# The convolution's pointwise weights multiplied with the output projection's lower half on the chip

## The chip, the cores and the metric

One core of a Trainium2 chip runs the whole layer as one program. TensorE multiplies matrices, VectorE (DVE) and ScalarE (ACT) do elementwise work, GpSimd (POOL) takes some of it, and DMA engines move data between HBM and the on-chip memories; SP, ScalarE and GpSimd issue transfers, each in its own order. The metric is the time of one execution of the program in microseconds (us). Before the change three runs took 2019.04, 2021.59 and 2022.71 us.

## The reference

One decoder layer over 2048 tokens of 1024 channels, in float32. A combined projection makes q, k, v and the input of a gated convolution; sliding-window attention and the convolution run side by side; their results are concatenated and go through one output projection; a SwiGLU feed-forward network follows. Norms stand around both halves. The part that the change touches:

```python
def conformer_conv(u, conv_dw, conv_dw_b, conv_ln_g, conv_ln_b, w_conv_pw):
    a, gate = jnp.split(u, 2, axis=-1)
    h = a * jax.nn.sigmoid(gate)
    h = lax.conv_general_dilated(h, conv_dw[:, None, :], ..., feature_group_count=D_CONV) + conv_dw_b
    h = jax.nn.silu(layer_norm(h, conv_ln_g, conv_ln_b))
    return h @ w_conv_pw
...
mixed = jnp.concatenate([attn_out, conv_out], axis=-1) @ w_out
h = h + rms_norm(mixed, mix_post_g)
```

`w_conv_pw` is 512 x 512, `w_out` 1024 x 1024. Its upper 512 rows meet the attention's output, its lower 512 rows the convolution's.

## The kernel before

**Precision.** Every float32 operand of a product is split into a high part (a copy to fp32r, on ScalarE) and a low part (the difference, on VectorE or GpSimd). `three` issues three products for each pair: high by high, high by low, low by high. `split_w` (L129) is the helper for weights. A tile of the kind "hl" or "chl" holds both parts of a 128 x 512 block.

**Stages.** The tokens are four tiles of 512 (t = 0 to 3). For each tile there are: A (the projections, 14 units of 24 products), B (attention), T (the 31 convolution taps, on VectorE), C (the convolution's tail) and W (the output projection, the norm and the residual). The feed-forward network treats two tiles at a time by a Strassen-like scheme: F0 and G0 for tiles 0 and 1, F2 and G2 for tiles 2 and 3. In the trace the letter after "@" is the stage.

**What sets the order.** One stage at a time runs as the main one; others are pumped beside it from lanes (`Lane`), each with a rate in units of the main stage's own clock. Lane `ld` holds the tails C0 and C1, and lane `lw` holds C2, W2, C3 and W3, which run beside G0. A scheduler then orders the instructions of each engine once, when the program is built, by priority and by its own estimate of time. On the chip each engine works through its list strictly in that order, and an instruction that waits holds up all that follow it on its engine. This holds for SP's list of transfers too.

**Buffers.** Tiles of one kind share a fixed number of buffers (`BUFS`, L53): 8 "hl", 3 "fc", 2 "gb", 1 "wx", 1 "yt", 5 "chl". A tile that is asked for waits until an earlier one is read for the last time. In PSUM there are four banks "mm", three "tr" and one "ct"; all of the tail's work goes through "ct".

**The tail** (`conv_tail`, L592). After the LayerNorm, four blocks of channels are turned (four transposes each), then activated: tanh (L613), scale and shift (L615), and one VectorE instruction (L616) that leaves twice the swish. Each is split (L618 on ScalarE, L619 on GpSimd). Then for each of four output blocks m the pointwise weights are loaded (L625) and split, 12 products go into "ct" (L628), ScalarE halves the result (L630) and stores it from its own queue to `mixT` (L631), from which W loads it (L715).

**The output projection** (`stage_w`, L697) takes the eight blocks of `mixT` in four groups of two, and loads and splits the weights `w_out` for each; W0 also stores their low parts (`lo_out`), which the other three load.

**Norms of the next tiles.** In A1, `row_norms` (L264) loads eight blocks of 128 rows of x (tiles 2 and 3) into buffers of the kind "hl" (L271), squares and sums them on ScalarE (L272), and computes the inverse root on VectorE and GpSimd (`rsqrt`, L159 to L162). `norm_x` (L289) spreads this over a diagonal (L301, tile "gb"), turns it on TensorE (L306), and `split_x` makes A2's operands, of the kind "hl" again. The hooks at L402 say after which unit of A1 each of these is emitted.

Of the kernel before, what the change touches and what calls it, by code (L numbers as in the profile page):

```python
# [12 lines left out]
F32 = mybir.dt.float32  # L13
F32R = mybir.dt.float32r
# [3 lines left out]
AF = mybir.ActivationFunctionType  # L18
ALU = mybir.AluOpType
# [4 lines left out]
D = 1024  # L24
DFF = 2816
P = 128
T = 512
# [10 lines left out]
def layer_kernel(ctx, tc, x, xT, cols, rows, sinks, relb, onehot, w_in, w_pw, w_out, w_gate, w_up, w_down, out):  # L38
    nc = tc.nc
# [4 lines left out]
    dr = ctx.enter_context(tc.tile_pool(name="dr", bufs=1, space=DRAM))  # L44

    uid = [0]
    lab = ["X0"]

    def nm(s):
        uid[0] += 1  # L50
        return f"{s}@{lab[0]}_{uid[0]}"
# [3 lines left out]
    def t_(tag, shape, dt=F32):  # L55
        return sb.tile(list(shape), dt, tag=tag, name=nm(tag), bufs=BUFS[tag])

    def f4(tag, shape=(P, D)):
        return t_(tag, shape)

    def f2(tag, shape=(P, T)):
        return t_(tag, shape)

    def hl(tag):
        return t_(tag, (P, 2, T), F32R)

    def sm(n, dt=F32):
        kind = "A" if lab[0][0] == "G" else lab[0][0]
        return sb.tile([P, 8], dt, tag="sm" + kind, name=nm("sm"), bufs={"C": 8, "W": 4}.get(kind, 16))[:, 0:n]

    def bank(tag, bufs):
        return ps.tile([P, T], F32, tag=tag, name=nm(tag), bufs=bufs)
# [3 lines left out]
    ct = lambda: bank("ct", 1)  # L76


    act = nc.scalar.activation
# [23 lines left out]
    ptt = nc.gpsimd.tensor_tensor  # L103
# [3 lines left out]
    def mat(*args, **kw):  # L107
        r = nc.tensor.matmul(*args, **kw)  # L108
        if not inlane[0]:
            lead_pe[0] = r  # L110
        return r
# [17 lines left out]
    def split_w(raw, tag, low=None, made=False, on_pool=True):  # L129
        w = tag if not isinstance(tag, str) else hl(tag)  # L130
        if made:
            nc.sync.dma_start(w[:, 1].bitcast(F32), low)
        act(w[:, 0], raw, AF.Copy)  # L133
        if not made:
            (ptt if on_pool else vtt)(w[:, 1], raw, w[:, 0].bitcast(F32), ALU.subtract)
            if low is not None:
                (nc.gpsimd if on_pool else nc.sync).dma_start(low, w[:, 1].bitcast(F32))
        return w

    def weight(src, low, made, raw=None, on_pool=True):  # L140
        if raw is None:
            raw = t_("raw", (P, 2, T))
            nc.sync.dma_start(raw, src)
        return [split_w(raw[:, n], "w", low[n], made, on_pool) for n in range(2)]
# [43 lines left out]
    def three(o, pairs, first=True, last=True):  # L188
        n = 3 * len(pairs)
        i = 0  # L190
        for (sh, sl), (mh, ml) in pairs:
            for a, b in ((sh, mh), (sh, ml), (sl, mh)):
                mat(o, a, b, start=first and i == 0, stop=last and i == n - 1)
                i += 1
# [34 lines left out]

    mixT = dr.tile([KC, P, S], F32, name="mixT")  # L230
    h_scr = dr.tile([S, D], F32, name="h_scr")

    neg = cst.tile([P, 1], F32, name="neg")
    nc.vector.memset(neg, NEG)
# [15 lines left out]
    started = set()  # L250
# [292 lines left out]
    def conv_in(t, c):  # L543
        g = t_("glu", (P, 576))[:, 0 : HALO + T]
        if t == 0:
            nc.vector.memset(g[:, 0:HALO], 0.0)
            nc.sync.dma_start(g[:, HALO:], glu_scr[c, :, 0:T])
        else:
            nc.sync.dma_start(g, glu_scr[c, :, t * T - HALO : (t + 1) * T])
        y = f2("fc")  # L550
        vts(y, g[:, 0:T], dwh[:, c, 0:1], dwb[:, c : c + 1], ALU.mult, ALU.add)
        return g, y
# [10 lines left out]
    def stage_taps(t):  # L563
        L = f"C{t}"
        for c in range(4):
            while f"g{t}{c}" not in started:
                yield None
            lab[0] = L
            g, y = conv_in(t, c)
            for j in range(1, TAPS):  # L570
                stt(y, g[:, j : j + T], dwh[:, c, j : j + 1], y, ALU.mult, ALU.add)
                yield 0.68
                lab[0] = L
            nc.sync.dma_start(y_scr[c, :, t * T : (t + 1) * T], y)
            yield 0.68
# [16 lines left out]
    def conv_tail(t, yt):  # L592
        L = f"C{t}"
        lab[0] = L
        mv = sm(8).rearrange("p (s a) -> p s a", a=2)
        for s in range(4):
            st = sm(6)
            nc.vector.bn_stats(st, yt[:, s])
            nc.vector.bn_aggr(mv[:, s], st)
        r = rsqrt(mv[:, :, 1], 4, 1.0)  # L600
        nmr = sm(4)
        stt(nmr, mv[:, :, 0], -1.0, r, ALU.mult, ALU.mult)
        yield YL if t < 2 else YL2
        lab[0] = L
        for s in range(4):
            act(yt[:, s], yt[:, s], AF.Identity, scale=r[:, s : s + 1], bias=nmr[:, s : s + 1])
        sc = []
        for c in range(4):
            b = ct()
            for s in range(4):  # L610
                nc.tensor.transpose(b[:, s * P : (s + 1) * P], yt[:, s, c * P : (c + 1) * P], ident)
            th = f2("fc")
            act(th, b, AF.Tanh, scale=lnh[:, c : c + 1], bias=lnh[:, 4 + c : 5 + c])  # L613
            v = f2("fc")
            act(v, b, AF.Identity, scale=ln_g[:, c : c + 1], bias=ln_b[:, c : c + 1])  # L615
            stt(v, th, 1.0, v, ALU.add, ALU.mult)  # L616
            h = hl("chl")
            act(h[:, 0], v, AF.Copy)  # L618
            ptt(h[:, 1], v, h[:, 0].bitcast(F32), ALU.subtract)  # L619
            sc.append(h)  # L620
            yield 2
            lab[0] = L
        for m in range(4):
            raw = f2("fc")
            nc.sync.dma_start(raw, w_pw[m])  # L625
            w = split_w(raw, "mb" if t == 1 and m % 2 else "chl").rearrange("p a (k c) -> p a k c", c=P)
            o = ct()
            three(o, [((w[:, 0, k], w[:, 1, k]), (sc[k][:, 0], sc[k][:, 1])) for k in range(4)])  # L628
            z = f2("gb" if t > 1 else "fc")
            act(z, o, AF.Copy, scale=0.5)  # L630
            nc.scalar.dma_start(mixT[4 + m, :, t * T : (t + 1) * T], z)  # L631
            yield 2
            lab[0] = L

    bias = []

# [60 lines left out]
    def stage_w(w, spill, G, atag, htag, mtag, bank_of, norm=None, ready=None):  # L697
        L = f"W{w}"
        lab[0] = L
        acc = [f4(atag) for _ in range(4)]  # L700

        def acts(gi, ms=None):
            aa = []
            for m in ms or load(gi):
                a = hl(htag)
                act(a[:, 0], m, AF.Copy)  # L706
                vtt(a[:, 1], m, a[:, 0].bitcast(F32), ALU.subtract)
                aa.append([a])
            return aa

        def load(gi):
            ms = []
            for c in range(G * gi, G * gi + G):
                ms.append(f2(mtag))
                nc.sync.dma_start(ms[-1], mixT[c, :, w * T : (w + 1) * T])  # L715
            return ms

        first = load(0)
        if w != 1:
            yield 5.0  # L720
            lab[0] = L
        nxt = acts(0, first)
        for gi in range(KC // G):
            aa = nxt
            for n in range(2):
                lab[0] = L
                if n == 0 and w != 1 and gi + 1 < KC // G:
                    rows_next = load(gi + 1)
                if n == 1 and gi + 1 < KC // G and not (ready and G * gi + G == 4):
                    nxt = acts(gi + 1, rows_next if w != 1 else None)  # L730
                ws = weight(w_out[2 * gi : 2 * gi + 2, :, n * T : (n + 1) * T].rearrange("c p t -> p c t"),
                            lo_out[n, 2 * gi : 2 * gi + 2], w > 0)
                yield from block_half(acc, list(zip(aa, ws)), n, gi == 0, L, bank_of)
            if ready and G * gi + G == 4:
                for i, c in enumerate(ready()):
                    if i == Q0 // 2:
                        ld.until("C1")
                        lab[0] = L
                        nxt = acts(gi + 1)
                    yield c  # L740
        tail = norm_w(w, spill, acc, mtag)
        if norm:
            norm(tail)
        else:
            yield from tail
# [601 lines left out]
    ld = Lane(2.0, 0)  # L1347
# [23 lines left out]
    hn_a = {0: split_x(0, x0, None, range(KC))}  # L1371
    for t in range(NT):
        lc.add(f"T{t}", stage_taps(t))
    for t in range(2):
        ld.add(f"C{t}", stage_tail(t), lambda t=t: since(lc, f"T{t}", CS))
    for t in range(NT):
# [38 lines left out]
    ws, ops = (0, 1), {}  # L1415
# [12 lines left out]
    ws, ops = (2, 3), {}  # L1428
# [76 lines left out]
```

## Time and profile before

| | |
|---|---|
| runs | 2019.04, 2021.59, 2022.71 us; median 2021.59 |
| span of the profiled execution | 2016.4 us |
| instructions | 27154 |
| TensorE busy | 1957.8 us, 97% |
| VectorE busy | 1489.5 us, 74% |
| ScalarE busy | 985.7 us, 49% |
| GpSimd busy | 355.0 us, 18% |

The span runs from the program's first instruction to its last; the time of the profiled execution itself is not listed beside it. A row of a stretch reads: the stretch, its length, then for each engine (TensorE's products, its weight loads, VectorE, ScalarE, GpSimd) the busy time and in brackets the number of instructions, then the granted clock of TensorE as a share, the share of the DMA engines' time, and GB/s; an engine that did nothing, or that was not asked for, is missing. A row of a timeline reads: start, time, engine, line, operation, what is written from what, how many, and in square brackets the idle time before it and what ended it. A row of a line or a tile has the shortest, median and longest duration in ns, then the first and last start. A row of waits has the total, the number and the longest. A row of transfers has their number, their size, and the median time from issue to landing.

### The profile page before, as it was taken

How to read it: one execution, taken by the hardware profiler on the slowest of the kernel's cores; microseconds unless marked ns; L12 is line 12 of the kernel's file. 1: busy time of each engine (PE TensorE's matmuls, PEld its weight loads, DVE VectorE, ACT ScalarE, POOL GpSimd, SP SyncE). 2: the span in 40 equal slices, each digit the busy share in tenths (PEclk: the TensorE clock that was granted, in tenths of full speed). 3: DMA queues.
4: the chain of work that ended last, by engine and by line, in shares of the span. 5: the costliest groups of instructions: out<-in, count | busy, mean ns of one | idle time of the engine just before them, and what ended most of it. 6: DMA issues, size and time to landing. Idle time of an engine off the chain costs nothing. (4 is left out here: it accounts for less than half of the span.)

```text
span 2016.4 us, 27154 instructions
## 1 busy us (share of the span) xinstructions
PE 1957.8 (97%) x8826; PEld 1563.3 (78%) x8826; DVE 1489.5 (74%) x2679; ACT 985.7 (49%) x1938; POOL 355.0 (18%) x415
## 2 busy tenths in 40 slices
PE   8999999999998999999989999999899999999998
PEld 7877767677667778888878878778688888888886
DVE  5998987985794899888569984475766765545558
ACT  5455455457546633333355466456643343345543
POOL 6000223322110300000001022103523332221000
PEclk9999999999999999999989999999999999999999
DMA  8786645669559878777476778579944443366654
GB/s 309 267 298 221 207 148 175 194 228 322 180 178 325 281 238 269 253 253 254 149 239 216 238 261 283 173 262 348 333 159 167 157 160 107 107 238 214 200 187 162
DMA packets 234110, 451.44 MB, mean 224 GB/s; under 512 B 23496, under 2 KB 49264, under 8 KB 233968
## 3 DMA queue, kind: packets, MB, share of 16 engines
q1 hardware_dynamic: 211184, 411.96, 60.9%
q10 hardware_dynamic: 20544, 30.42, 4.1%
q0 software_dynamic: 2240, 7.34, 0.9%
q8 instruction: 69, 1.13, 0.2%
q14 instruction: 73, 0.60, 0.1%
HBM read 330.60 MB, written 119.02 MB: 223 GB/s over the span
## 5 line engine op out<-in xcount | busy, mean ns | idle before, releaser
L85 DVE SCALAR_TENSOR_TENSOR fc@C<-glu@C,colt,fc@C 128x512 f32<-128x512 f32 x480 | 367.8, 780 | 3.0
L108 PE MATMUL mm@F<-hl@H,w@F 128*128 128x512 f32 x1056 | 254.9, 392 | 5.3 <-ACT mm@F L924 4.9
L108 PEld LDWEIGHTS mm@F<-hl@H,w@F 128*128 128x128 f32 x1056 | 198.5, 189 | 48.8 <-ACT mm@F L924 6.7
L108 PE MATMUL mm@G<-hl@G,hl@G 128*128 128x512 f32 x924 | 228.0, 396 | 6.4 <-DVE x@G L85 4.3
L108 PE MATMUL mm@A<-hl@A,w@A 128*128 128x512 f32 x840 | 206.3, 396 | 3.0 <-ACT hl@A L318 1.2
L108 PEld LDWEIGHTS mm@G<-hl@G,hl@G 128*128 128x128 f32 x924 | 174.1, 190 | 44.5 <-issue 4.1
L797 ACT ACTIVATE w@F<-chl@F 128x512 fp32r<-128x512 f32 x220 | 135.6, 625 | 135.3 <-PE mm@F L108 123.3
L108 PE MATMUL mm@G<-w@G,hl@G 128*128 128x512 f32 x876 | 199.5, 389 | 0.0
L108 PEld LDWEIGHTS mm@G<-w@G,hl@G 128*128 128x128 f32 x876 | 164.4, 188 | 34.1
L108 PEld LDWEIGHTS mm@A<-hl@A,w@A 128*128 128x128 f32 x840 | 154.7, 188 | 39.4 <-DVE hl@A L85 3.0
L85 DVE TENSOR_TENSOR w@F<-chl@F,w@F 128x512 fp32r<-128x512 f32 x198 | 144.9, 733 | 34.7 <-ACT w@F L797 34.3
L108 PE MATMUL mm@F<-mid@H,w@F 128*128 128x512 f32 x528 | 131.1, 393 | 7.4 <-ACT mm@F L924 7.2
L108 PE MATMUL mm@F<-p@H,w@F 128*128 128x512 f32 x528 | 129.1, 389 | 0.8 <-ACT at@F L1046 0.8
L108 PE MATMUL mm@F<-ql@H,w@F 128*128 128x512 f32 x528 | 127.2, 389 | 0.7 <-ACT w@F L797 0.7
L108 PE MATMUL mm@F<-x@H,w@F 128*128 128x512 f32 x528 | 125.5, 391 | 0.0
L108 PEld LDWEIGHTS mm@F<-mid@H,w@F 128*128 128x128 f32 x528 | 98.3, 188 | 30.2 <-ACT mm@F L924 9.0
L108 PEld LDWEIGHTS mm@F<-p@H,w@F 128*128 128x128 f32 x528 | 98.9, 188 | 21.9 <-ACT at@F L1046 1.4
L108 PEld LDWEIGHTS mm@F<-ql@H,w@F 128*128 128x128 f32 x528 | 99.0, 188 | 21.6 <-ACT w@F L797 1.1
L108 PEld LDWEIGHTS mm@F<-x@H,w@F 128*128 128x128 f32 x528 | 98.7, 188 | 21.0
L108 PE MATMUL tr@W<-w@W,ql@W 128*128 128x512 f32 x384 | 103.0, 408 | 8.4 <-ACT ql@W L706 5.1
L133 ACT ACTIVATE w@A<-raw@A 128x512 fp32r<-128x512 f32 x110 | 67.7, 626 | 78.8 <-PE mm@A L108 51.5
L108 PE MATMUL mm@W<-w@W,hl@W 128*128 128x512 f32 x384 | 101.5, 404 | 2.2 <-ACT x@W L679 0.7
(302 smaller groups left out, 3337.0 us busy)
## 6 DMA issues: line engine op xcount, KB each, us to landing
mids<-fa@F SPq DMA_DIRECT2D x154, 256.0 KB, 2.7
raw@A<-w_in SPq DMA_DIRECT2D x55, 512.0 KB, 4.4
w@A<-lo_in SPq DMA_DIRECT2D x84, 256.0 KB, 3.5
fc@G<-mids SPq DMA_DIRECT2D x77, 256.0 KB, 3.5
fa@G<-mids SPq DMA_DIRECT2D x75, 256.0 KB, 4.5
gb@F<-keeps SPq DMA_DIRECT2D x72, 256.0 KB, 4.3
raw@W<-w_out SPq DMA_DIRECT2D x32, 512.0 KB, 5.5
w@W<-lo_out SPq DMA_DIRECT2D x48, 256.0 KB, 4.4
```

Source lines behind the costliest of these rows:

```text
L85: r = op(*args, **kw)
L108: r = nc.tensor.matmul(*args, **kw)
L133: act(w[:, 0], raw, AF.Copy)
L797: act(w[:, 0], x, AF.Copy)
```

## The change

Instead of applying the pointwise weights to every tile's activated rows, the program multiplies them once with the lower half of `w_out`; the result, halved, is kept in DRAM as `w_join`. The tails store the activated rows in `mixT` without a product, and W takes `w_join` in place of `w_out`'s lower half. The pointwise weights are handed over transposed. The new stage J is the first item of lane `ld`, ahead of C0, and begins when A1 has begun.

```diff
+    w_join = dr.tile([4, P, D], F32, name="w_join")
...
@@ conv_tail
-        sc = []
         for c in range(4):
...
             stt(v, th, 1.0, v, ALU.add, ALU.mult)
-            h = hl("chl")
-            act(h[:, 0], v, AF.Copy)
-            ptt(h[:, 1], v, h[:, 0].bitcast(F32), ALU.subtract)
-            sc.append(h)
+            nc.sync.dma_start(mixT[4 + c, :, t * T : (t + 1) * T], v)
             yield 2
             lab[0] = L
+
+    def stage_join():
+        lab[0] = "J0"
+        right = []
+        for k in range(4):
+            raw = f4("wx", (P, 2, T))
+            nc.sync.dma_start(raw, w_out[4 + k].rearrange("p (a b) -> p a b", a=2))
+            yield 1.5
+            for n in range(2):
+                lab[0] = "J0"
+                right.append(split_w(raw[:, n], "hl"))
+            yield 1.5
+            lab[0] = "J0"
         for m in range(4):
-            raw = f2("fc")
+            if m % 2 == 0:
+                pair_ = t_("yt", (P, 2, 2, T), F32R)
+            raw = f2("gb")
             nc.sync.dma_start(raw, w_pw[m])
-            w = split_w(raw, "mb" if t == 1 and m % 2 else "chl").rearrange("p a (k c) -> p a k c", c=P)
-            o = ct()
-            three(o, [((w[:, 0, k], w[:, 1, k]), (sc[k][:, 0], sc[k][:, 1])) for k in range(4)])
-            z = f2("gb" if t > 1 else "fc")
-            act(z, o, AF.Copy, scale=0.5)
-            nc.scalar.dma_start(mixT[4 + m, :, t * T : (t + 1) * T], z)
-            yield 2
-            lab[0] = L
+            yield 1.5
+            lab[0] = "J0"
+            left = split_w(raw, pair_[:, m % 2]).rearrange("p a (k c) -> p a k c", c=P)
+            yield 1.5
+            for n in range(2):
+                lab[0] = "J0"
+                o = ct()
+                three(o, [((left[:, 0, k], left[:, 1, k]), (right[2 * k + n][:, 0], right[2 * k + n][:, 1])) for k in range(4)])
+                z = f2("gb")
+                act(z, o, AF.Copy, scale=0.5)
+                nc.scalar.dma_start(w_join[m, :, n * T : (n + 1) * T], z)
+                yield 4
+                lab[0] = "J0"
...
@@ stage_w
-                ws = weight(w_out[2 * gi : 2 * gi + 2, :, n * T : (n + 1) * T].rearrange("c p t -> p c t"),
+                src = w_out[2 * gi : 2 * gi + 2] if gi < 2 else w_join[2 * gi - 4 : 2 * gi - 2]
+                ws = weight(src[:, :, n * T : (n + 1) * T].rearrange("c p t -> p c t"),
...
+    ld.add("J", stage_join(), lambda: "A1" in started)
     for t in range(2):
         ld.add(f"C{t}", stage_tail(t), lambda t=t: since(lc, f"T{t}", CS))
...
-    wp = kblocks(f(w_conv_pw))
+    wp = kblocks(f(w_conv_pw).T)
```

The join's eight groups are numbered by m (four) and n (the two halves of 512 columns): the seventh is m = 3, n = 0. All groups of one n use the same four of the eight split pairs `right`.

## The prediction

> **What bounds the kernel now.** I read the page first (busy shares and the chain that ended last), then the windows.
>
> ```profile
> PE 1957.8 (97%) x8826; PEld 1563.3 (78%) x8826; DVE 1489.5 (74%) x2679; ACT 985.7 (49%) x1938; POOL 355.0 (18%) x415
> ...
> PE 38%; DMA 5%; DVE 3%; ACT 1%; issue 1%; POOL 0%; SPq 0%; DVEq 0%; ACTq 0%
> ```
>
> TensorE (PE) is busy nearly all of the span, and the chain spends 38% of it there. Matmuls overlap, so a busy PE need not be a full one; three windows of 50 us settle that.
>
> ```profile
> 150.00:200.00 50.00, 50.00 (x252) 38.02 (x250) 43.99 (x99) 26.83 (x71) 3.90 (x4) 1.00 0.66 213
> ...
> 1100.00:1150.00 50.00, 49.04 (x215) 39.81 (x214) 49.79 (x74) 20.37 (x38) 4.59 (x3) 1.00 0.70 226
> 1550.00:1600.00 50.00, 50.00 (x222) 41.42 (x221) 33.30 (x43) 20.25 (x36) 16.76 (x11) 1.00 0.46 162
> ```
>
> The last row is pure FFN: 222 products of 128x512 in 50 us, 225 ns each. That is the price of a product in a full stretch. In the first row (projections A1 and A2, with attention's small products between) and in the second (first down projection, G0, with C2 and W2 beside it) TensorE is as full, but VectorE (third pair) is at 44 and 49.8 of 50: a second engine stands close behind.
>
> **What is removed.** Each tail multiplied its four activated blocks by the pointwise weights, 4 x 12 products; four tails make 192.
>
> ```profile
> L108 PE MATMUL ct@C<-chl@C,chl@C x168: 388/389/795, 288.1 to 1274.0; 128*128 128x512 f32 x168
> ...
> L108 PE MATMUL ct@C<-chl@C,mb@C x24: 387/392/502, 499.2 to 525.3; 128*128 128x512 f32 x24
> ...
> L619 POOL TENSOR_TENSOR chl@C<-fc@C,chl@C x16: 1281/1298/2978, 264.3 to 1238.8; 128x512 fp32r<-128x512 f32 x16
> ```
>
> 168 + 24 = 192 products at 225 ns: -43.2 us. Around the first two tails they also cost stalls, and a lower granted clock after them:
>
> ```profile
> 286.00:288.00 2.00, 0.97 (x9) 1.00 0.75 255
> 288.00:290.00 2.00, 1.57 (x5) 0.94 0.64 228
> 290.00:292.00 2.00, 2.00 (x7) 0.50 0.75 192
> 292.00:294.00 2.00, 2.00 (x8) 0.71 0.04 8
> ```
> ```profile
> 508.00:510.00 2.00, 1.70 (x5) 0.55 0.67 243
> 510.00:512.00 2.00, 2.00 (x7) 0.60 0.03 8
> ```
>
> From 288 to 294 stand 20 products where 6 us hold 26.7 (1.5 us lost); from 508 to 512 12 of 17.8 (1.3 us). With about 1 us idle at 286 that is up to 4 us that go with the products, but what then comes earlier may wait itself: I take -3 (0 to -4).
>
> Not on the path: the splits of blocks and weights. ScalarE is half idle. On GpSimd 32 subtractions of 1.3 us go (16 of them in the last row above) and 12 come; only what they do to VectorE counts:
>
> ```profile
> 264.31 1.28 POOL L619 TENSOR_TENSOR chl@C<-fc@C,chl@C 128x512 fp32r<-128x512 f32 x1 [14.09 <-ACT chl@C L618]
> ```
> ```profile
> 265.63 0.55 DVE L85 TENSOR_SCALAR fc@C<-glu@C,colt 128x512 f32<-128x512 f32 x1 [2.24 <-POOL chl@C L619]
> ...
> 269.38 0.69 DVE L85 SCALAR_TENSOR_TENSOR fc@C<-fc@C,fc@C 128x512 f32<-128x512 f32 x1 [1.64 <-ACT fc@C L615]
> ...
> 273.52 0.75 DVE L85 SCALAR_TENSOR_TENSOR fc@C<-glu@C,colt,fc@C 128x512 f32<-128x512 f32 x1
> ```
>
> VectorE sat 2.24 us behind one subtraction of 1.28. This matters in C2. There VectorE is full, so 48 x 225 ns = 10.8 us taken from TensorE alone would be lost again; with eight subtractions gone VectorE gets back something between nothing and 8 x 1.28 = 10.2 us. I take 2 us lost of the 10.8 (0 to 10.8). The Trainium skill (SBUF — State Buffer, section "SBUF: two separate sides") says that GpSimd and a VectorE operation with two SBUF inputs hold one port pair in turn, for a whole instruction. By that rule all 10.2 us come back and the sum below would be 2 us lower.
>
> C3 ends in a chain of latencies, store of the product, then its load by W3:
>
> ```profile
> 1249.38 4.14 DMA mixT<-gb@C
> 1253.58 3.47 DMA at@W<-mixT
> ```
> ```profile
> PE tr@W L108 <- ACT ql@W L706: 3.1, 2, 2.1
> ```
>
> After the change these rows are in memory before W3 begins. What TensorE waits for them goes: -2 (0 to -4).
>
> **What is added.** The join makes 4 x 2 groups of 12 products: 96 x 225 ns = +21.6. It runs in A1, which is full on both engines (first window row), so nothing hides it. Its eight stores go out on ScalarE's queue; W0 reads them two projection stages later.
>
> **What is moved.** The tails' 16 stores leave ScalarE's queue for SP's, where each waits for its VectorE instruction (0.69 us above), with weight loads behind it. These loads run three steps ahead: 0. The sixteen pointwise loads on SP become four, and four half-megabyte loads of the output weights come.
>
> Now the order of the changed program, which names no times. The join keeps eight of the eight "hl" buffers from A1's start. The same buffers took the eight row loads of x from which A2's and A3's norms come. On SP these loads stood early in A1; now the first four wait for the join's seventh group (m = 3, first half) to free its pairs, and the last four for the Squares of the first four. And TensorE's order is: v projection, attention's last block with the join's sixth and seventh groups, **the first transpose of A2's norm**, then the q projections. TensorE works in order: nothing can pass that transpose.
>
> ```profile
> L271 SPq DMA_DIRECT2D hl@A<-x x8: 328/358/488, 91.0 to 104.2; - x8
> ...
> DMA to landing us min/median/max: 3.3/9.2/10.9
> ```
> ```profile
> L272 ACT ACTIVATE junk<-hl@A x8: 1041/1058/1062, 94.4 to 115.2; 128x1024 bf16<-128x1024 f32 x8
> L272 ACT ACTIVATION_READ_ACCUMULATOR junk<-hl@A x8: 185/187/189, 95.3 to 116.1; 128x1 f32 x8
> ```
> ```profile
> 116.14 0.19 ACT L272 ACTIVATION_READ_ACCUMULATOR junk<-hl@A 128x1 f32 x1
> ...
> 118.15 0.39 ACT L478 ACTIVATE p@B<-p@B,sm@B 128x128 f32<-128x128 f32 x1
> ...
> 118.24 0.20 POOL L159 TENSOR_TENSOR sm@A<-sm@A 128x8 f32<-128x8 f32 x1 [64.10 <-DVE sm@A L85]
> ```
> ```profile
> 123.44 0.88 DVE L85 TENSOR_SCALAR gb@A<-ident,sm@A 128x128 f32<-128x128 f32 x4 [0.60 <-POOL sm@A L162]
> ```
> ```profile
> 163.27 0.60 PE L306 MATMUL mm@A<-ident,gb@A 128*128 128x128 f32 x4
> ...
> 192.21 3.00 PE L108 MATMUL mm@A<-hl@A,w@A 128*128 128x512 f32 x12
> ```
> ```profile
> L133 ACT ACTIVATE w@A<-raw@A 128x512 fp32r<-128x512 f32 x110 | 67.7, 626 | 78.8 <-PE mm@A L108 51.5
> ...
> raw@A<-w_in SPq DMA_DIRECT2D x55, 512.0 KB, 4.4
> ```
>
> Before, the diagonal was ready at 123.4 and used at 163.3, 29 us ahead of A2's first product (192.2): 40 us of cover. That cover is gone. Count from the third product of the seventh group (T). First load: issue 0.36, landing 4.4 (what 512 KB took as weights), at 4.8; Square and read 1.25, at 6.0. The fourth pair comes free with the group's last product, about T+3 with attention's transposes between; lands 7.8; fourth Square ends at 9.8 at the latest. The eighth load waits for it: 0.36 + 4.4 + 1.25, at 15.8. From the last read's end (116.33) to the diagonal (123.44) the trace has 7.1: T+22.9. TensorE is through with what stands before the transpose (nine products, 2.0 us, and some twelve small ones of attention) at T+5. Hole: 17.9, say 17, since VectorE has no taps left to put between.
>
> Ahead of it the seventh group itself waits: its weights' load stands on SP behind one that waits for a split after the v projection. From that projection's end, two splits 1.2, two issues 0.7, landing 4.4, split and subtraction 1.9, with eight of attention's exponentials (0.39 each, 3 us) between on ScalarE: 11 us, against 6 to 7 of TensorE work. That adds 4. Sum of the hole: +21. With landing 3.3 and no wait ahead it is 15; with 9.2, 34.
>
> After an idle stretch the granted clock falls:
>
> ```profile
> 1328.00:1330.00 2.00, 0.42 (x4) 1.00 0.53 183
> ...
> 1332.00:1334.00 2.00, 1.65 (x4) 0.50 0.49 190
> 1334.00:1336.00 2.00, 2.00 (x6) 0.50 0.80 201
> 1336.00:1338.00 2.00, 2.00 (x7) 0.59 1.06 408
> ```
>
> 17 products in 6 us instead of 26.7: 2.2 us lost. I take +2 for one such dip (1 to 4.4, two of them). The Trainium skill (TensorE: Matmul & The Clock Gate, section "What's actually happening") has the clock halved after an idle window of about 3.4 us and for one busy window; by this rule the wait of 4 ahead of the hole would bring a dip of its own, and the sum would be 2 higher.
>
> **Sum**: -43.2 - 3 + 2 - 2 + 21.6 + 21 + 2 = -1.6 on a span of 2016.4: 2014.8. Median and span differ by 2021.6 - 2016.4 = 5.2, so the forecast is **2020**, no change: the halved product is paid back by one hole. With all terms at their ends it lies between -13.6 and +27.6, or 2008 and 2049.
>
> **The rivals.**
>
> *The hole stays small* (chance 0.20). If the seventh group runs earlier than I place it, so that the chain passes under it, or the rows land at once, the gain comes through: -43.2 - 3 + 2 - 2 + 21.6 = -24.6, or with a rest of 4 of the hole, **2001**. For it: TensorE waits little anywhere now. Against it: the order is fixed, and eight loads, eight Squares and a norm stand between two neighbours on TensorE.
>
> *A1's loads land late* (0.27), slower. The join's four blocks of output weights pass one by one through the single "wx" buffer: each round is issue and landing 4.8, split 0.6, two subtractions 2.6. Three rounds after the first are 24 us, while TensorE has some 24 us of work before the join's first product (96 products, 21.6, and attention's first block). So every us of landing over 4.4 stalls TensorE three times, and the hole twice more. At 7 us, between 4.4 and the 9.2 that A1's row loads took, that is 5 x 2.6 = 13: **2033**. It decides from about 5 us.
>
> *VectorE is the bound* (0.13): C2's whole 10.8 and half of C0's are lost, 9 + 5 more: **2034**. For it the row at 1100; against it the subtractions that go.
>
> **How the numbers follow.** The forecast keeps 0.40; its own spread is 8 us to either side, since its largest terms nearly cancel. What a measurement of this kernel can tell from no change is about 0.2%, 4 us. Of the 0.40, faster gets 0.12, same 0.18, slower 0.10. The first rival adds 0.20 to faster, the others 0.37 to slower and 0.03 to same: 0.32, 0.21, 0.47. The range, 2004 to 2040, leaves out about half of the first rival and the tail of the two slow ones.
>
> **What would show it.** Right: no product on the bank "ct" in the C stages; 96 in A1 at 225 ns; TensorE idle 13 to 20 us in one piece late in A1, ended by the diagonal (VectorE), the eight Squares just before it, the granted clock at 0.5 after it; A2 begins some 43 us later than at 192, and G0 is 15 us or more shorter. Wrong: the transposes of A2's norm without a wait of over 8 us before them (then the first rival); waits of the join's first product for its subtractions (the second); G0 as long as before with VectorE full in it (the third).

## The result and the profile after

Four runs of the changed kernel took 2029.65, 2039.21, 2041.91 and 2043.10 us, median 2040.56, against 2022.15 (four runs) for the kernel before on the same chip: a ratio of 1.0087, interval 1.0060 to 1.0115. It is 0.9% slower, 18 us by the medians, where no change was forecast. The profiled execution took 2041.91 us with a span of 2040.2, 23.8 longer than before. From its page:

```profile
PE 1959.2 (96%) x8730; PEld 1558.3 (76%) x8730; DVE 1488.0 (73%) x2679; ACT 970.2 (48%) x1910; POOL 319.4 (16%) x395
...
PE 46%; DVE 9%; DMA 8%; issue 2%; ACT 1%; POOL 0%; SPq 0%; DVEq 0%; ACTq 0%
```

There are 96 products fewer, and yet TensorE is busy as long: a product that runs slowly or at half clock counts as busy for longer. VectorE and transfers have a larger part of the chain than before. Windows cut at the first product of A1, A2, A3, W1 and F0 place the loss; first the kernel before, then the changed one (columns as above; the last three are the granted clock, the DMA share and GB/s):

```profile
95.50:192.20 96.70, 96.70 (x481) 73.77 (x480) 88.05 (x216) 48.94 (x122) 6.96 (x15) 1.00 0.80 274
192.20:309.10 116.90, 114.02 (x560) 84.27 (x559) 104.60 (x236) 63.49 (x168) 24.34 (x27) 0.99 0.55 175
309.10:472.40 163.30, 162.21 (x768) 118.98 (x767) 140.32 (x290) 84.58 (x195) 54.25 (x80) 1.00 0.67 221
472.40:593.60 121.20, 112.65 (x535) 79.89 (x534) 90.52 (x209) 67.52 (x162) 15.24 (x16) 0.99 0.61 208
```
```profile
96.10:253.20 157.10, 135.22 (x602) 98.73 (x600) 117.12 (x249) 65.50 (x163) 23.49 (x29) 0.91 0.59 197
253.20:357.50 104.30, 104.30 (x520) 77.61 (x518) 82.78 (x210) 55.15 (x141) 8.42 (x19) 1.00 0.63 203
357.50:520.60 163.10, 160.21 (x740) 117.08 (x739) 144.46 (x292) 80.46 (x187) 44.88 (x66) 0.99 0.66 214
520.60:633.50 112.90, 103.37 (x482) 73.19 (x481) 84.59 (x206) 60.49 (x150) 12.01 (x20) 0.94 0.64 213
```

A1 grew from 96.7 to 157.1. Summed by stage, with the prediction's terms and with the first experiment (the row loads ahead of the join, below) beside it, in us of span against the kernel before. Each column is one profiled execution, so its sum need not equal the difference of the medians: that of "rows first" took 2016.41 us, the second longest of ten, where the median is 2012.01.

| | predicted | changed | rows first |
|---|---|---|---|
| start to A1 | 0 | +0.6 | +0.7 |
| A1 (21.6 products, 21 hole, 2 clock) | +44.6 | +60.4 | +27.7 |
| A2 to W1's end (C0, C1) | -24.6 | -21.1 | -16.2 |
| F0 | 0 | +7.1 | +4.2 |
| G0 (C2, C3) | -21.6 | -21.0 | -16.2 |
| F2, G2 | 0 | -2.2 | -1.9 |
| sum | -1.6 | +23.8 | -1.7 |

Inside A1, the waits of TensorE and windows of 10 us:

```profile
PE mm@A L307 <- DVE gb@A L85: 15.8, 1, 15.8
PE tr@B L108 <- DVE sm@B L460: 2.9, 2, 2.2
PE tr@B L108 <- ACT p@B L502: 2.4, 1, 2.4
PE tr@B L501 <- DVE p@B L85: 0.7, 2, 0.6
```
```profile
170.00:180.00 10.00, 10.00 (x41) 5.89 (x39) 7.11 (x12) 5.11 (x17) 2.55 (x2) 1.00 0.66 206
180.00:190.00 10.00, 10.00 (x23) 5.54 (x23) 1.69 (x10) 0.60 (x1) 0.00 (x0) 0.66 0.36 129
190.00:200.00 10.00, 8.02 (x46) 6.10 (x44) 2.61 (x14) 6.17 (x23) 0.64 (x1) 1.00 0.42 133
200.00:210.00 10.00, 7.98 (x36) 3.67 (x36) 9.75 (x14) 4.91 (x9) 4.36 (x4) 1.00 0.57 193
...
220.00:230.00 10.00, 5.18 (x13) 4.12 (x14) 1.39 (x7) 0.89 (x3) 2.43 (x12) 0.50 0.07 26
```

The forecast hole is there: one wait of 15.8 us, then a clock of 0.50. But time is lost earlier too. From 180 to 190 TensorE has no idle time and yet only 23 instructions, about half of what the windows around it hold. The timeline shows why (start, duration):

```profile
180.07 0.50 PE L108 MATMUL ct@J<-hl@J,yt@J 128*128 128x512 f32 x1
180.50 0.38 PE L108 MATMUL tr@B<-kz,ql@A 64*128 64x256 f32 x1
...
183.51 0.79 PE L108 MATMUL ct@J<-hl@J,yt@J 128*128 128x512 f32 x1
184.23 0.58 PE L108 MATMUL tr@B<-kz,ql@A 64*128 64x256 f32 x1
...
207.90 1.08 PE L108 MATMUL tr@B<-p@B,vd@B 128*64 128x512 f32 x4
224.82 0.47 PE L307 MATMUL mm@A<-ident,gb@A 128*128 128x128 f32 x1 [15.84 <-DVE gb@A L85]
```

The join's fifth group and attention's score products alternate one by one: 0.74 us from one join product to the next (180.07 to 180.81), and 1.23 from about 182.3 on, at half clock. The hole ends, as forecast, with a chain of loads and Squares:

```profile
L272 SPq DMA_DIRECT2D hl@A<-x x8: 327/328/328, 204.5 to 214.2; - x8
```

Before the change these loads were issued from 91.0 to 104.2.

### The profile page after: what moved, and what is told of

Same layout as the page of the kernel before. It is cut to its first block, busy times and chain, and to the rows that moved or that the text cites. A ratio compares the mean times of both kernels' runs of the same rounds, so it can differ in the third digit from the quotient of the medians.

```text
span 2040.2 us, 26930 instructions
## 1 busy us (share of the span) xinstructions
PE 1959.2 (96%) x8730; PEld 1558.3 (76%) x8730; DVE 1488.0 (73%) x2679; ACT 970.2 (48%) x1910; POOL 319.4 (16%) x395
## 4 chain that ended last, share of the span: by engine, by line
PE 46%; DVE 9%; DMA 8%; issue 2%; ACT 1%; POOL 0%; SPq 0%; DVEq 0%; ACTq 0%
PE mm@F L108 29%; PE mm@G L108 14%; PE tr@W L108 2%; DVE fc@C L85 2%; DVE hl@G L85 1%; DMA gb@F<-keeps 1%; DVE mid@W L85 1%; DVE w@F L85 1%; DMA chl@F<-w_gate 1%; DMA at@W<-mixT 1%; DMA chl@F<-w_up 1%; DMA fa@G<-mids 1%; DMA mixT<-fc@C 1%; DMA fc@G<-w_down 1%; DVE fa@F L85 1%
## 5 line engine op out<-in xcount | busy, mean ns | idle before, releaser
L108 PEld LDWEIGHTS mm@F<-p@H,w@F 128*128 128x128 f32 x528 | 98.9, 188 | 21.1 <-ACT at@F L1064 0.6
L108 PEld LDWEIGHTS mm@F<-x@H,w@F 128*128 128x128 f32 x528 | 98.8, 188 | 20.7
```

## The experiments

Twelve kernels were run. The chips' times of the kernel before lie between 2019.99 and 2022.86 (medians), so ratios are compared, each with its interval.

**1. The row loads ahead of the join.**

```diff
                 row_norms([t] if t == 1 else [2, 3], "p" if t == 1 else "hl")
+                started.add(f"n{t}")
-    ld.add("J", stage_join(), lambda: "A1" in started)
+    ld.add("J", stage_join(), lambda: "n2" in started)
```

> The join may only start after the eight row loads of x for A2's and A3's norms have taken their buffers; nothing else differs from the changed kernel. Theory (the rows of x stand behind the join for its buffers, so the norm is late): the 15.8 us of idle time before the first transpose of A2's norm goes, and the 2.7 us of half clock behind it, so A2 starts about 18 us earlier than 253, and the time is about 2022 (2016 to 2027). Rival 1 (the hole only shows that A1's loads and VectorE cannot carry more): the wait moves to the join's own products or to A2's splits, A2 starts at 245 or later, time 2034 to 2041. Rival 2 (nothing but the hole costs in A1): A2 starts at 214 to 220 and the time is below 2005.

Measured: 2012.01 us (ten runs), 0.9956 (0.9940 to 0.9972): slightly faster than the kernel before, and 26 us below the changed kernel (1.0087 - 0.9956). A1 in one window, and the loads:

```profile
96.20:220.60 124.40, 122.41 (x599) 91.49 (x597) 116.48 (x244) 64.44 (x161) 29.36 (x30) 1.00 0.73 248
```
```profile
L272 SPq DMA_DIRECT2D hl@A<-x x8: 327/355/892, 92.6 to 107.2; - x8
```

TensorE waits 2.0 us in all of A1, and the clock stays at 1.00. Not only the hole went: A2 starts 32.6 us earlier, where hole and half clock behind it are 18.5. With the norm in time the groups stand at other places, and the alternation and most of the smaller waits are gone too. So A1's loss beyond the products comes, all but a few us, from the order in which join and row loads take the buffers: A1 is 27.7 us longer than before, for 21.6 us of products. The cause named by the theory is right, its size is not: A2 was to start 18 us earlier, and its start lies at the edge of rival 2 (214 to 220). The time is 4 us below the theory's range and 7 above rival 2.

**2. Join and attention kept apart on TensorE.**

```diff
+    turn_ = [None, None]
+    def apart(kind, r):
+        if turn_[0] is not None and turn_[0] != kind:
+            after_first(turn_[1], r)
+        turn_[:] = [kind, r]
+        return r
...
-                mat(o, a, b, ...)
+                r = mat(o, a, b, ...)
+                if kind:
+                    apart(kind, r)
```

The join calls `three` with `kind="J"`, the score products in B go through `apart("B", ...)`.

> The join's products and attention's 64-row score products are told not to pass into each other: a group begun is finished first. Nothing else differs from the changed kernel, the hole included. Theory (12 pairs of a join product and a score product, one after the other at 0.74 us and partly at half clock, where 0.31 would do, cost 5 to 7 us in 176 to 187): TensorE has no such stretch, time about 2034 (2031 to 2037). Rival (what stands behind them waits for other engines anyway): 2039 to 2042, the stretch replaced by idle time.

Measured: 2052.98, 1.0162 (1.0141 to 1.0184); its profiled execution, 2046.51, is the fastest of four. Slower than the changed kernel: the theory falls, and its rival was too mild. The alternation is gone, and A1 takes 159.5 us instead of 157.1; the idle time of TensorE in it (gaps over 0.1 us, added up) rises from 21.9 to 28.4. The join's groups now wait for their weights' split and for the single bank "ct" (1.7 and 2.5 us at the longest), attention for VectorE. So the alternation was slow, but it filled waits, and keeping the two apart saved nothing.

**3 and 4. Each half of the change alone.** The tails without the join, and the join beside the old tails:

```diff
-                src = w_out[2 * gi : 2 * gi + 2] if gi < 2 else w_join[2 * gi - 4 : 2 * gi - 2]
+                src = w_out[2 * gi : 2 * gi + 2]
...
-    ld.add("J", stage_join(), lambda: "A1" in started)
```

> The tails' half of the change without the join: the tails store activated rows, and the output projection multiplies them with the unjoined weights, so the pointwise weights are left out of the computation. Theory (the tails give what was forecast, and A1 alone was priced too low): 41 to 47 us below the kernel before, about 1978 (1973 to 1983). Rival 1 (VectorE bounds C2, so part of the 10.8 us of its products does not come back): 1985 to 1990. Rival 2 (the loss sits in the tails' stores on SyncE's queue): 1995 or more.

> The join added to the kernel before, its result stored and not read; tails and output projection as before. Theory (the join costs about 60 us where it stands, whatever the tails do): about 2081 (2075 to 2088), A2 starts near 253. Rival 1 (the join costs what the prediction's terms for A1 say, 21.6 + 21 + 2): about 2067, and the rest of the loss belongs to the tails. Rival 2 (its products alone): 2044.

Measured: the tails alone 1993.21, 0.9873 (0.9856 to 0.9890), a gain of 28 (26 by the ratio) and not of 41 to 47; the join alone 2075.23, 1.0281 (1.0258 to 1.0303), a loss of 54. The join's theory holds, at the lower edge of its range (A2 starts at 255.5). For the tails the time lies between the two rivals, and the first names the wrong place: G0 became 27.8 us shorter, more than forecast, while A1 to W1 stayed as it was (before 498.1, here 497.7), with 96 products fewer. The second, the stores on SyncE's queue, was not tested by itself: between 255 and 475 SP waits 13.4 us at these stores (L617), and no run tells what that costs. The whole stretch before, then with the tails alone, followed by A2, A3 and W1 of the latter:

```profile
95.50:593.60 498.10, 485.58 (x2338) 356.90 (x2337) 423.50 (x949) 264.54 (x646) 100.79 (x138) 0.99 0.65 218
```
```profile
97.20:594.90 497.70, 472.53 (x2242) 344.83 (x2241) 418.54 (x952) 251.92 (x623) 81.70 (x122) 0.97 0.66 213
...
193.90:303.60 109.70, 106.74 (x535) 78.48 (x533) 98.34 (x224) 57.10 (x145) 15.65 (x22) 1.00 0.59 184
303.60:475.00 171.40, 161.29 (x750) 117.65 (x749) 143.05 (x307) 85.08 (x206) 46.57 (x68) 0.97 0.65 201
475.00:594.90 119.90, 107.80 (x483) 74.92 (x482) 88.68 (x207) 60.73 (x151) 12.81 (x18) 0.90 0.64 207
```

What TensorE no longer did came back as waiting (25.2 us instead of 12.5) and as a lower clock (in W1 0.90 instead of 0.99). Of C0's products 7.2 us were gained in A2 (109.7 instead of 116.9), and more than that was lost in A3 (171.4 instead of 163.3), mostly in two waits, for ScalarE at W0's first product and for VectorE in attention:

```profile
326.01 0.50 PE L108 MATMUL mm@W<-w@W,hl@W 128*128 128x512 f32 x1 [4.09 <-ACT hl@W L723]
...
396.59 1.97 PE L108 MATMUL tr@B<-p@B,vtok 128*64 128x512 f32 x4 [4.45 <-DVE sm@B L460]
```

Before the change W0's first product (333.4) waited 0.3 us, with twelve of C0's products from 324.0 on shortly before it. Where C1's products stood, the timeline of before shows what they had covered, the transposes of the feed-forward's operands (tr@H); below it the same place in the changed kernel:

```profile
495.62 0.60 PE L815 MATMUL tr@H<-ident,fa@H 128*128 128x128 f32 x4
...
499.19 0.73 PE L108 MATMUL ct@C<-chl@C,mb@C 128*128 128x512 f32 x2
500.54 2.58 PE L108 MATMUL ct@C<-chl@C,mb@C 128*128 128x512 f32 x10 [0.62 <-POOL mb@C L135]
502.96 1.47 PE L815 MATMUL tr@H<-ident,fa@H 128*128 128x128 f32 x12
506.96 0.66 PE L815 MATMUL tr@H<-ident,fa@H 128*128 128x128 f32 x4 [2.52 <-ACT gb@H L835]
...
509.46 3.56 PE L108 MATMUL ct@C<-chl@C,chl@C 128*128 128x512 f32 x10 [0.30 <-POOL chl@C L135]
...
513.29 0.60 PE L815 MATMUL tr@H<-ident,fa@H 128*128 128x128 f32 x4
```
```profile
541.07 0.63 PE L833 MATMUL tr@H<-ident,fa@H 128*128 128x128 f32 x4 [0.90 <-DMA fa@H<-hn_scr]
543.88 1.70 PE L833 MATMUL tr@H<-ident,fa@H 128*128 128x128 f32 x8 [2.18 <-DVE sm@B L460]
...
551.96 1.95 PE L833 MATMUL tr@H<-ident,fa@H 128*128 128x128 f32 x8 [3.77 <-DMA fa@H<-hn_scr]
...
557.79 0.42 PE L833 MATMUL tr@H<-ident,fa@H 128*128 128x128 f32 x1
```

From the start of the first of these transposes to that of the last group it is 17.7 us before (495.6 to 513.3, with 24 of the tail's products among them) and 16.7 after (541.1 to 557.8, with none). Those 24 products had cost about 1 us there, not 5.4.

**5. The join in A2, in other buffers.**

```diff
-                right.append(split_w(raw[:, n], "hl"))
+                right.append(split_w(raw[:, n], "mid" if k < 2 else "chl"))
...
-    ld.add("J", stage_join(), lambda: "A1" in started)
+    ld.add("J", stage_join(), lambda: "A2" in started)
```

> The join starts with A2 instead of A1, and its pairs stand in the eight buffers that A1's normed rows have just left ('mid' and 'chl'), not in those of the row loads; the tails as in the changed kernel. Theory (A1's 60 us come from the buffers shared with the row loads, and from the work that piles up in front of the late norm, not from the products): A2 starts at 192 to 196 as before the change, no idle time over 4 us before a norm's transpose, and since TensorE lost the first two tails' 24 us between A2 and W1, where VectorE is busy 482 of 498 us with the tails alone, part of the 21.6 us is hidden: W1 ends 1 to 12 us later than before, time 2000 to 2012. Rival 1 (the products cost their 21.6 us wherever they stand): W1 ends 20 to 25 us later, time 2017 to 2022. Rival 2 (any place makes a late norm): a hole of over 10 us before A3's norm, time 2025 or more.

Measured: 2006.22, 0.9912 (0.9892 to 0.9932), the fastest version that leaves nothing out of the computation. A2 starts at 193.2, no wait over 2.3 us in A1 or A2, W1 ends 13.9 later. The first theory's time holds, and W1 came 2 us later than it allows. A2 with the join took 135.8 us, where it took 116.9 before, with C0's products in it, and 109.7 with the tails alone. From A1 to W1 it is 511.0 us against 497.7 with the tails alone: 13.3 of the join's 21.6 are paid there, the rest is covered.

**6, 7 and 8. Less work for VectorE.** In the first two tiles ten taps are left out, in the kernel before (6), with the tails alone (7) and with the join behind the row loads (8):

```diff
+                if t > 1 or j < TAPS - 10:
                     stt(y, g[:, j : j + T], dwh[:, c, j : j + 1], y, ALU.mult, ALU.add)
```

> The kernel before with the last 10 of 30 taps left out of the convolution of the first two tiles (80 of VectorE's instructions at 0.69 us, 55 us of its 487 between A1's start and W1's end), as the measure for the next run. Both theories: 2005 to 2021, the less gained the more TensorE is the other bound of that stretch.

> The tails without the join (the pointwise weights left out of the computation) and the same 80 taps left out as in the run beside it. Theory (with the tails alone the time from A1 to W1 stayed at 498 us, because VectorE was busy 482 of them: the 96 products of the first two tails were covered): with 55 us less of VectorE's work the products count, A1 to W1 is 20 us or more shorter than in the run beside it, and the time is 43 to 52 us below it, where it was 28 without that. Rival (waits in the attention's chain or late loads keep that stretch long): the difference stays at 25 to 32.

> The changed kernel with the row loads ahead of the join, and the same 80 taps left out. Theory (VectorE bounds A1 to W1): compared with the kernel before with the same taps left out, the time is 20 to 26 us lower, near the 24.6 us that the products alone were forecast to give, where it was 9 with all taps. Rival (the join's own waits keep the rest): 5 to 12 lower.

The 482 and 487 us in these texts add up VectorE's instructions, which overlap; as the windows count, it was busy 418.5 of 497.7 and 423.5 of 498.1 us. So "VectorE bounds" says too much: it is nearly full in some stages only. Measured: 2036.74 (1.0061, 1.0038 to 1.0085), 1987.36 (0.9821, 0.9800 to 0.9842) and 2005.31 (0.9926, 0.9899 to 0.9954). A1 to W1 with fewer taps, first the kernel before, then the tails alone:

```profile
98.00:602.40 504.40, 491.01 (x2337) 359.29 (x2337) 372.15 (x867) 264.68 (x647) 88.24 (x138) 0.99 0.66 213
```
```profile
97.80:582.00 484.20, 471.25 (x2241) 343.94 (x2240) 365.51 (x869) 252.88 (x623) 73.86 (x122) 0.98 0.67 217
```

With VectorE at 74 to 76% the products count: 20.2 us between the two, where it was 0.4 with all taps, and 49 us in all. That speaks for the theory, with a reservation: run 6 was outside its own range, 14 us slower than with all taps, so less work made a worse order. Of the 20.2, 13.5 are a real gain of run 7 over run 3; 6.3 are what run 6 lost, and 0.4 were there before. Run 8 lies 31 us below run 6, beyond both ranges; its A1 to W1 took 509.6 us, as in run 1, so VectorE was not what held run 1 there.

**9. Four row loads behind the join instead of eight.**

```diff
-                row_norms([t] if t == 1 else [2, 3], "p" if t == 1 else "hl")
+                row_norms([t], "p" if t == 1 else "hl")
+                rn.setdefault(3, rn[t])
```

> The changed kernel with A2's row loads alone behind the join: four loads instead of eight, and A3 uses A2's norm (its own is left out of the computation). Theory (the hole is the prediction's chain: buffers freed by the seventh group, loads, one Square after another, 7 us of norm, diagonal): in the changed kernel the fourth Square was through at 214.2 and the eighth at 220.4, so the hole of 15.8 us shrinks by 6.2 to 9 to 10 us, and A2 starts near 247, time 2033 to 2036. Rival (the loads land late whatever their number, or the norm waits for another engine): the hole stays at 14 to 17 us.

Measured: 2036.34, 1.0068 (1.0038 to 1.0098), and the hole is 12.5 us, between the two expectations. The chain's last part, in this kernel and in the changed one:

```profile
214.53 0.19 ACT L273 ACTIVATION_READ_ACCUMULATOR junk<-hl@A 128x1 f32 x1
...
216.53 0.68 POOL L159 TENSOR_TENSOR sm@A<-sm@A 128x4 f32<-128x4 f32 x1 [7.96 <-DVE sm@A L85]
217.29 0.71 POOL L160 TENSOR_TENSOR sm@A<-sm@A,sm@A 128x4 f32<-128x4 f32 x1
...
219.65 0.20 POOL L159 TENSOR_TENSOR sm@A<-sm@A 128x4 f32<-128x4 f32 x1
...
221.84 0.87 DVE L85 TENSOR_SCALAR gb@A<-ident,sm@A 128x128 f32<-128x128 f32 x4 [2.32 <-POOL sm@A L162]
222.18 0.47 PE L307 MATMUL mm@A<-ident,gb@A 128*128 128x128 f32 x1 [12.48 <-DVE gb@A L85]
```
```profile
220.22 0.19 ACT L273 ACTIVATION_READ_ACCUMULATOR junk<-hl@A 128x1 f32 x1
...
221.11 0.20 POOL L159 TENSOR_TENSOR sm@A<-sm@A 128x8 f32<-128x8 f32 x1 [13.27 <-DVE sm@A L85]
...
224.47 0.68 DVE L85 TENSOR_SCALAR gb@A<-ident,sm@A 128x128 f32<-128x128 f32 x3 [3.45 <-POOL sm@A L162]
```

The Squares were through 5.7 us earlier (214.7 against 220.4; 6.2 expected). But now VectorE still had taps, and the norm took 7.1 us to the diagonal instead of 4.1; TensorE came to the hole 0.7 us later, too. So the hole is 3.4 us shorter: it is this chain, link by link.

**10 and 11. The join in A2 with slower taps, or spread wider.** From run 5, `RC1` 1.1 to 0.8, or the rate of the item J from 2.0 to 1.0.

> The join in A2 as in the run before, and the second tile's taps at 0.8 of a us of VectorE's work per us of the projections' instead of 1.1. Theory (with the join in A2 the stage took 135.8 us because VectorE had 146 us of instructions in it, taps above all, while W0 and W1 had room): A2 takes 122 to 130 us, W1 ends 5 to 9 us later than before the change instead of 13.9, time 1998 to 2003. Rival (TensorE bounds A2 with the join in it, 117 + 21.6): A2 stays at 133 or more, and time 2004 to 2010; if the late taps hold up the second tail, more.

> The join in A2 at half the rate, spread over the whole stage; taps as they were. Theory (VectorE bounds A2): nothing to gain, 2003 to 2010. Rival (what the join costs in A2 are its own waits and the crowding at its start): 1 to 8 us lower than with the faster join, 1998 to 2005.

Measured: 2015.94 (0.9970, 0.9954 to 0.9986) and 2010.78 (0.9945, 0.9922 to 0.9968), neither better than run 5. A2 took 136.1 and 134.9 us. Run 10's theory falls; for A2 its rival holds, with the join in it TensorE sets the length. The time is 6 us above the rival's range. The late taps did not hold up W1, which ends 1.5 us earlier than in run 5; F2 and G2 took 657.7 us in the profiled execution instead of 649.2, and why is open. Run 11 ends 1 us above its theory's range: spreading the join gains nothing.

**12. The join behind the row loads, beside the old tails.** Edits 1 and 4 together.

> The kernel before with the join added, its result stored and not read, and the join held back until the row loads of x for A2's and A3's norms have their buffers. It differs from the join alone by that order only. Theory (what the lateness of the norm costs is 28 us, as between the changed kernel and the same with the rows first, whatever the tails do): 2044 to 2050, where the join alone took 54 us more than the kernel before. Rival 1 (the tails' products and the join's collide in A2 once A2 comes early, so that less is won back): 2053 to 2065. Rival 2 (VectorE alone bounds A1 to W1, and the join's 21.6 us are covered as the tails' were): 2030 to 2040.

Measured: 2055.02, 1.0172 (1.0150 to 1.0194). The lateness of the norm costs 22 us beside the old tails (1.0281 - 1.0172) and 26 beside the new (1.0087 - 0.9956): rival 1, if not by much. And beside a join that waits for nothing the tails bring 44 us (1.0172 - 0.9956), where alone they brought 26 (1 - 0.9873): from A1 to W1 it is 20.7 us (530.3 against 509.6) instead of 0.4. That the join's products fill there what the tails' had filled is a reading that fits this, not shown by itself.

## Why the prediction was wrong

By the table the sum missed by 25.4 us: 15.8 in A1, 7.1 in F0, 3.5 in A2 to W1, and -1.0 in the rest. The 3.5 hide two larger errors that nearly cancel.

**The hole was right.** It stands where the prediction put it, at the first transpose of A2's norm, 15.8 us against 17, ended by the diagonal, the eight Squares just before. From the seventh group's third product (done at about 204.4) to the diagonal (224.47) the chain took 20 us against 22.9: the loads and Squares 16.0 against 15.8, the norm 4.1 against 7.1, with no taps beside it. Run 9 confirms it link by link, and run 1 that the order of the buffers makes it. The wait ahead of it was 3.0 (2.4 and 0.6) against 4; TensorE waited there for attention's copy on ScalarE, behind the eight exponentials of the forecast, and not for the group's weights, whose loads landed in 2.2 us (median) and not in 4.4. The half clock behind it cost 2.7 against 2 (twelve products in 5.4 us, from 224.94). Together 21.5 of 23 forecast. (The hole's upper end, 34, comes by its own parts to about 35: 21, and three times 4.8 for landings of 9.2.)

**One step that failed is "192 products at 225 ns: -43.2", taken in full.** In G0 it held: -21.0 against -21.6, with C2's VectorE and C3's waits. That it came out so near is in part luck, since with the same tails G0 gained 16 us in run 1 and 33 in run 10. From A2 to W1 the first two tails were to give 24.6 (21.6 and stalls of 3). Alone they gave 0.4 (run 3): those products had filled waits, C0's ahead of W0's first product and C1's among the transposes of the feed-forward's operands, and what they left was idle time and half clock. In the changed kernel the stretch is 21.1 us shorter, but 6.4 of that come with the late A2 alone (run 4 has them, with the old tails: 395.0 us from A2 to W1's end instead of 401.4). So 14.7 are the tails', if the two add up: 10 too few. The prediction costed this loss only as a rival, and in VectorE alone.

**The other, and the larger in the sum, is "96 x 225 ns = +21.6" in A1, without a price for the company.** The 60.4 us of A1 are: 21.6 of products; 21.5 of hole, wait ahead and clock behind, as forecast; about 5 of attention's work moved up from A2 (28 value products lie in A1 instead of 12, at 0.27 us, and eight transposes more), which A2 gives back; and some 12 that the prediction did not have: 3.1 of waits around the first groups (121 to 136), about 1.6 of half clock behind the longest of them (4.2 us from 134.4 on, with 2.4 of work in it), about 7 where the fifth group alternates with attention's products (174.7 to 189.3, 14.6 us with 7 of work in it), and a small rest. Run 2 shows that the alternation can't be forbidden at a gain; run 1 that it goes with the order of the buffers.

**F0 was counted as 0** and took 7.1 us more (3.9 with the tails alone, 0 with the join alone). Of these 4.3 are idle time of TensorE (13.2 us instead of 8.9); no run was made for it, and its cause is open. So is why G0 gained 28 and 29 us in runs 3 and 5, but 16 in run 1, where TensorE waits 20.6 us in it and 14.0 in run 3.

**The rivals.** The hole stays small (2001): run 1 is that case, and gave 2012. The net of the products, 24.6 less, on which it and the forecast rest, was 9 (0.9956), and 18 with the join in A2 (run 5). A1's loads land late, 2033: its time was near, but its mechanism not what happened. Its condition was met, since the join's loads of the output weights landed in 4.0 to 7.2 us (median 5.9) and the rows in 5.2, yet no wait of the join's first group for its subtractions is among A1's waits. VectorE is the bound: G0 was not as long as before, so it falls where it was placed; in A2 to W1 run 7 speaks for a part of it.

**The clock and the port pair.** By the Trainium skill (TensorE: Matmul & The Clock Gate, section "What's actually happening"), which has the clock halved after an idle window of about 3.4 us, a wait of 4 ahead of the hole was to bring a dip of its own. It was 2.4 us long, and the clock stayed at 1.00 there. But in run 9 the same wait, at the same place and of the same length, was followed by half clock; first the changed kernel, then run 9:

```profile
200.00:202.00 2.00, 1.58 (x8) 0.40 (x8) 2.00 (x5) 1.36 (x3) 1.36 (x2) 1.00 0.14 54
```
```profile
200.00:202.00 2.00, 1.63 (x4) 0.53 (x6) 2.00 (x5) 1.32 (x3) 1.41 (x2) 0.51 0.16 61
```

The changed kernel's wait of 2.2 us before 134.4 was followed by 0.51, too (136 to 138). All these waits are shorter than that window, so its length alone does not tell here whether a dip comes. The Trainium skill (SBUF — State Buffer, section "SBUF: two separate sides"), by which GpSimd and a VectorE operation with two SBUF inputs hold a port pair in turn, agrees with run 9: GpSimd's small operations took 0.68 to 0.71 us beside the taps and 0.20 after them. Whether it gave back all of C2's 10.8 us, no run separates.

## What to carry to other kernels

Before work is put into a stage, list whose buffers it takes and what stands behind these on the same queues: here the order of two items was worth 26 us, while the change with the better order brought 9. Products taken from a busy engine count only where no wait is hidden beneath them: look at what stands between them in the engine's order, and at what that waits for. Work added to a full engine can cost more than its own time where it alternates with work of another shape.

## What the runs showed of the hardware

A 128-row product that alternates with a 64-row one took 0.74 us a pair at full clock, where in closed groups the two take 0.225 and 0.08 us (twelve score products in 0.97 us). And the granted clock fell to 0.66 in a window (180 to 190) in which TensorE shows no idle time, only few instructions: pairs then took 1.23 us. The trace shows no idle stretch ahead of this dip (the ends of products are modelled, so short gaps between them could be hidden). A wait's length did not decide either: behind a wait of 2.4 us at the same place the clock was at 1.00 in the changed kernel and at 0.51 in run 9.
